# Storing a split projection weight to DRAM one tile sooner in the first token quarter

## The chip, the cores and the metric

The kernel runs on one core of one Trainium2 chip. The metric is device time in microseconds; lower is better. Before the change it takes 2681.71 us, the median of three runs (2680.83 to 2684.74).

## The reference

One decoder layer over 2048 tokens with a width of 1024, in fp32. A combined input projection feeds four gated-DeltaNet heads and four HGRN2 heads; their outputs go through an output projection, then an MLP and an embedding gate. The part that matters here is the projection and what is made of it:

```
hn   = rms_norm(h, pre_mix_norm)
proj = einsum('btd,dc->btc', hn, w_in)          # 1024 x (32 blocks of 128, and 8 decay columns)
qkv  = silu(causal_conv(proj[qkv]))              # gated DeltaNet: q, k, v, z, and decay a, b
f, i, q, g = proj[hgrn]                          # HGRN2: forget, input, query, gate
o_a  = gated_delta_rule(q, k, v, decay, beta)    # 4 heads
o_b  = hgrn2(silu(q), (1 - lb) sigmoid(-f), i, log_f)   # 4 heads
h    = h + rms_norm(concat(o_a, o_b) @ w_out)
h    = h + rms_norm(relu(rms_norm(h) @ w_up)^2 @ w_down)
h    = h + rms_norm(p @ w_ple) * sigmoid(h @ w_gate)
```

## The kernel before, in words

Every fp32 matrix product is done as three products of "split" operands. A tile is split into a rounded copy (ScalarE, ACT, line 167) and the remainder (VectorE, DVE, line 168). A weight block of 1024 x 128 in both parts is a tile `w` of 1 MB in one of three buffers with the tag `whl`; its unsplit form `raw` is 0.5 MB in one of two buffers with the tag `raw`.

The projection and the two mixers run as a list of `works`, four quarters of 512 tokens each. A quarter has 33 works: work 0 is the small `ab` block (decay and beta), and then come eight weight blocks (k, q, v, z, f, i, query, g) for each of four head pairs. Work j is one output tile of 24 matmuls (line 1219), done in three parts of eight. After each part `tick()` runs what the `agenda` holds for that clock: steps of the mixers (`gdn_mixer`, `hgrn_mixer`), whose offsets are lists written out by hand (`A_STEPS`, `B_STEPS`, and `A_FIRST` for the first head). After the last part, `then` moves the product out of PSUM (`conv_silu`, `gate` with its tile `zt`, `fold`).

In the first quarter each weight block is loaded raw (`stage_work`, line 390) and split (`split_work`, lines 167 and 168). The split tile is also stored to DRAM (`keep_work`, which calls `keep`, line 183, tensor `cache_in`). In the three later quarters `split_work` reloads it from there (`reload`, line 188). At the head of step j the order is: split tile j+2, start the raw load of j+3, store tile j. So a `whl` buffer comes free for tile j+3 when PE has used tile j and the store of tile j has landed. The ab tile and the first raw loads are done ahead of the loop.

The order on TensorE (PE) is the program's (`manual_schedule` around the whole), and in this loop SyncE's (SP) too: SP issues all transfers, in one queue and in program order, and waits there for what each needs. The orders on ACT, DVE and GpSimd (POOL) are set by a planner, which weighs readiness by its own cost estimates.

The steps of a DeltaNet head that the prediction names: decay rows `gb` are stored (`gd`, line 640) and read back spread over the partitions (`gf`, line 744). From `gf` come `tail` (755), `e` (761, then 763 on ACT) and further exponentials. `u` goes through DRAM as `ud` (820) and comes back as `sys` (829); the small triangular solves make `xs` (840 to 845), stored as `xd` (850), read back as `xt` (857) and turned into `xn` (859); `psp`, `part`, `pst`, `psd` join the blocks (864 to 900), and `psa`, `psb`, `psc` carry the state `S` (906 to 918). In the HGRN2 head `keys` (1000) and `qk` (997) feed the `at` products (995).

Of the kernel before, what the change touches and what calls it, by code (L numbers as in the profile page):

```python
# [85 lines left out]
def trunk(ctx, tc, x, xT, pT, vecs, w_in, w_ab, gdn_a_log, gdn_dt_bias, w_out, w_up, w_down,  # L86
# [19 lines left out]
    def bank(name, pool=None):  # L106
        return (pool or pm).tile([P, QT], F32, tag="ps", name=name)

    def blk(c):
        return slice(c * P, (c + 1) * P)  # L110
# [69 lines left out]
    def keep(key, w):  # L180

        c = dr.tile([P, 2 * KD * P], F32, name=f"cache_{key}")
        nc.sync.dma_start(c, w.bitcast(F32).rearrange("p h k n -> p (h k n)"))
        cached[key] = c
# [67 lines left out]
    def tok(q):  # L252
        return slice(q * QT, (q + 1) * QT)
# [30 lines left out]
    def stage_ple(i, name, parts=1):  # L284

        raw = wp.tile([P, KD, P], F32, tag="raw", name=f"raw_{name}", bufs=2)
        n = 4 // parts

        def fetch(j):
            nc.sync.dma_start(raw[:, 2 * n * j : 2 * n * (j + 1)].rearrange("p (d k) n -> p d k n", k=2),  # L290
                              w_ple[4 * i + n * j : 4 * i + n * (j + 1)].rearrange("d p k n -> p d k n"))

        def ready(eng):
            w = wp.tile([P, 2, KD, P], F32R, tag="whl", name=f"w_{name}")
            for half in range(2):
                sl = slice(half * KD // 2, (half + 1) * KD // 2)
                split(w[:, :, sl], eng, raw[:, sl])
                if parts > 1:
                    between[half]()
            return w  # L300

        fetch(0)
        between = [lambda: None] * 2
        return (ready, partial(fetch, 1), between) if parts > 1 else ready
# [72 lines left out]
    def tick():  # L377
        for gen in agenda.pop(clock[0], ()):
            next(gen, None)
        clock[0] += 1  # L380

    def half():

        for gen in agenda.pop(clock[0] - 0.5, ()):
            next(gen, None)
# [184 lines left out]
    with mixers as mctx:  # L570
# [51 lines left out]
        def decays(ps, q):  # L622

            if q:
                gb = mt(f"gb_{q}", "gb", 1, (36, QT))
                rows = decay_rows(ps, gb, m2.tile([4, QT], F32, tag="tmp", name=f"sp_{q}"),
                                  m2.tile([4, QT], F32, tag="th", name=f"se_{q}"),
                                  lambda: tc.issue_after(turns[-1]))
                for _ in range(3):
                    next(rows)  # L630
                yield
                next(rows, None)
                gd = dr.tile([4, QT], F32, name=f"gd{q}")
                decay[q] = [gd, None]
                yield
                nc.sync.dma_start(gd, gb[0:4, :])
            else:
                gb, gd = first_gb, dr.tile([4, QT], F32, name="gd0")
                decay[q] = [gd, None]
                nc.sync.dma_start(gd, gb[0:4, :])  # L640
            yield
            back = mt(f"gbb_{q}", "gbb", 1, (36, QT // 2))
            V.tensor_copy(back.rearrange("p (n b i) -> p n b i", b=NB, i=SB), odd_back(gb))
            ps = bank(f"ps_gb_{q}", ph)
            for c in range(NC):
                PE.transpose(ps[:, c * 36 : (c + 1) * 36], back[:, blk(c // 2)] if c % 2 else gb[:, blk(c)],
                             ident[:36, :36])
            gcol = sm.tile([P, NC, 36], F32, tag="gcol", name=f"gcol_{q}", bufs=2)
            V.tensor_copy(gcol.rearrange("p c n -> p (c n)"), ps[:, : NC * 36])
            V.tensor_scalar(gcol[:, :, 4:8], gcol[:, :, 0:4], -1.0, None, ALU.mult)  # L650
            decay[q][1] = gcol

        def urgent(gen):

            done = False
            while not done:
                with tc.high_priority():
                    done = next(gen, gen) is gen
                yield
# [429 lines left out]
        works = []  # L1089

        def at(t, gen, offsets):
            for o in offsets:
                agenda.setdefault(t + o, []).append(gen)

        def call(t, fn):
            def once():
                fn()
                yield
            at(t, once(), (0,))
# [18 lines left out]
        def stage_work(j):  # L1118

            if j < len(works) and works[j][3] == 0:  # L1120
                staged[j] = stage(works[j][0], works[j][2])

        def split_work(j):

            if j < len(works):
                split_w[j] = staged.pop(j)() if j in staged else reload(works[j][1], works[j][0])

        def keep_work(j):
            if works[j][3] == 0:
                keep(works[j][1], split_w[j])  # L1130

        def load_x(q):
# [66 lines left out]
        with tc.manual_schedule(engines={mybir.EngineType.SP}):  # L1199
            assert [w[0] for w in works[:4]] == ["ab0", "4_0_0", "0_0_0", "8_0_0"]  # L1200
            for j, (name, key, src, q, h, then, g, b) in enumerate(works):
                if j:
                    split_work(j + 2)
                if j:
                    stage_work(j + 3)
                if j:
                    keep_work(j)
                ps = bank(f"mm_{name}", pp if j == 2 else None) if j else ps_ab
                w, xt = split_w.pop(j), xts[q]
                terms = []  # L1210
                for k, xk in enumerate(xt):
                    terms += [(w[:, 0, k, :], xk[:, 0, :]), (w[:, 0, k, :], xk[:, 1, :]), (w[:, 1, k, :], xk[:, 0, :])]
                nt = len(terms)
                for s in range(SPT):
                    for i in range(s * nt // SPT, (s + 1) * nt // SPT):
                        if i == (2 * s + 1) * nt // (2 * SPT):
                            half()
                        if j:
                            PE.matmul(ps, *terms[i], start=i == 0, stop=i == nt - 1)  # L1219
                    if s == SPT - 1 and h is None:  # L1220
                        at(clock[0], decays(ps, q) if q else urgent(decays(ps, q)), (0, 2.5, 3, 5) if q else (2, 6))
                    tick()
                    if s == SPT - 1 and h is not None:
                        then(ps, q, h, g, b)

            qs = (2, 3)
            ple = [stage_ple(i, f"pleb{i}") for i in range(2)]
            pts = {q: [operand(ra, pT[blk(k), tok(q)], f"pT{q}_{k}", stage=m2) for k in range(2)] for q in qs}
            ple = [w(V) for w in ple]
            fill = [(q, d) for q in qs for d in range(KD)]  # L1230
            store = None
            at(clock[0], mix_operands(0), (0, 1, 2, 3, 4, 6, 7, 9, 11))
            call(clock[0] + 2, partial(stage_out, 0))
            call(clock[0] + 5, partial(ready_out, 0))
            call(clock[0] + 6, partial(stage_out, 1))
            call(clock[0] + 13, partial(ready_out, 1))
            call(clock[0] + 14, partial(stage_out, 2))
            held = {}
            homes = (("ld", 2), ("tmp", 2), ("rsx", 1), ("ld", 2), ("th", 2))

            def first_outs():

                for j in range(2):
                    ps = held[j] = bank(f"mmo_0_{j}")
                    w = ready.pop(j)
                    for i in range(3 * KD):
                        k, term = i // 3, i % 3
                        PE.matmul(ps, w[:, term // 2, k, :], xin[0][k][:, term % 2, :], start=i == 0, stop=i == 3 * KD - 1)
                        if i % 8 == 7:
                            yield  # L1250

            outs = first_outs()
            while clock[0] <= last or len(held) < 2 or 1 in ready:
                if fill:
                    q, d = fill.pop(0)
                    new = embed_tile(q, d, ple[d // 4], pts[q], m2, *homes[len(fill) % len(homes)])
                    if store:
                        store()
                    store = new
                else:  # L1260
                    if store:
                        store()
                        store = None
                    next(outs, None)
                half()
                tick()
            for _ in outs:
                tick()
# [730 lines left out]
```

## Time and profile before

| | us |
|---|---|
| median of three runs | 2681.71 |
| the profiled execution | 2682.78 |
| its span, first to last instruction | 2681.0 |
| PE busy | 2643.5 (99%) |
| DVE busy | 2023.3 (75%) |
| ACT busy | 1499.5 (56%) |
| POOL busy | 106.4 (4%) |

The first quarter's works run on PE from about 38 to 280 us. All times inside the profile are counted from the span's start. In a line of waits, the three numbers are the total in us, how often, and the longest. In a line of the timeline, the first number is the start, the second the length, and in square brackets stands the engine's idle time just before and what ended it. In a line of windows come the stretch, its length, the busy times of PE, PEld, DVE, ACT and POOL with counts of instructions, the clock granted to PE, the DMA engines' busy share and GB/s.

### The profile page before, as it was taken

Reading aid. Unit: us, or ns where it says so; the run is one execution under the profiler, and the core shown is the slowest. Engines: PE = TensorE matmul, PEld = TensorE weight load, DVE = VectorE, ACT = ScalarE, POOL = GpSimd, SP = SyncE. Lnnn points to the kernel's source line nnn. Section 1 sums busy time; section 2 is a strip of 40 time slices with the busy share of each in tenths; the row PEclk is TensorE's granted clock in tenths of the full one; section 3 lists DMA queues with packets and bytes.
Section 4 is the critical chain, followed back from the end, with each engine's and each line's share of the span. In section 5 each row is a group of like instructions: output and inputs, shape, how many; then the busy total and the mean of one; then the engine's idle time right before and its main releaser. Section 6 shows DMA issues by size and latency. Waiting matters only on the chain.

```text
span 2681.0 us, 38473 instructions
## 1 busy us (share of the span) xinstructions
PE 2643.5 (99%) x12729; PEld 2206.1 (82%) x12729; DVE 2023.3 (75%) x4202; ACT 1499.5 (56%) x3174; POOL 106.4 (4%) x114
## 2 busy tenths in 40 slices
PE   8999999999999999999999999999999999999999
PEld 6888888888888888888888888887888888888887
DVE  6787777777787777478889977757788875668776
ACT  6665655465456456576566655545466664465322
POOL 0000000000000000000000000000000000001000
PEclk9999999999999999999999999999999999999999
DMA  8876777666656665877566676657465655677563
GB/s 282 273 260 216 235 257 231 220 209 243 214 201 222 219 219 176 296 276 276 176 217 219 214 240 222 211 195 252 140 235 178 206 194 191 196 252 254 191 223 133
DMA packets 268311, 594.11 MB, mean 222 GB/s; under 512 B 50250, under 2 KB 54824, under 8 KB 250704
## 3 DMA queue, kind: packets, MB, share of 16 engines
q1 hardware_dynamic: 268112, 591.65, 65.2%
q8 instruction: 101, 1.65, 0.3%
q14 instruction: 98, 0.80, 0.1%
HBM read 427.83 MB, written 163.70 MB: 221 GB/s over the span
## 4 chain that ended last, share of the span: by engine, by line
PE 65%; DVE 17%; DMA 10%; ACT 4%; issue 2%; POOL 1%; SPq 1%; POOLq 0%; DVEq 0%; ACTq 0%
PE u L1286 21%; PE d L1286 20%; PE mm L1219 10%; PE mmg L1286 6%; DVE pr_g L840 3%; PE mmo L1286 2%; DMA sys_g<-ud_g 2%; DVE xs_g L843 2%; DMA ud_g<-u_g 2%; DVE xs_g L845 2%; PE mme L194 1%; DMA rsb_g<-rd_g 1%; DMA da<-sumd 1%; DMA mixT<-mixd 1%; DMA raw_out<-in_w_out_dram 1%
## 5 line engine op out<-in xcount | busy, mean ns | idle before, releaser
L1219 PE MATMUL mm<-xt,w 128*128 128x512 f32 x3072 | 785.1, 401 | 4.1 <-ACT zt_zg L712 3.5
L1219 PEld LDWEIGHTS mm<-xt,w 128*128 128x128 f32 x3072 | 555.2, 189 | 108.1 <-ACT zt_zg L712 3.7
L1286 PE MATMUL d<-db,da 128*128 128x512 f32 x2688 | 611.3, 389 | 1.7 <-DVE db L221 1.6
L1286 PE MATMUL u<-t,wu 128*128 128x512 f32 x2604 | 592.8, 389 | 1.7 <-ACT wu L167 0.8
L1286 PEld LDWEIGHTS d<-db,da 128*128 128x128 f32 x2688 | 504.1, 188 | 108.2 <-DVE db L221 3.6
L1286 PEld LDWEIGHTS u<-t,wu 128*128 128x128 f32 x2604 | 488.5, 188 | 104.3 <-ACT wu L167 1.2
L221 DVE TENSOR_TENSOR db<-db 128x512 fp32r<-128x512 f32 x224 | 159.6, 713 | 70.6 <-ACT db L220 70.0
L220 ACT ACTIVATE db<-db 128x512 fp32r<-128x512 f32 x224 | 140.8, 629 | 78.4 <-DMA db<-hid 76.7
L1675 DVE TENSOR_TENSOR u<-u,u 128x512 f32<-128x512 f32 x224 | 150.2, 680 | 37.1 <-PE u L1286 36.3
L1716 ACT ACTIVATE u<-u 128x512 f32<-128x512 f32 x128 | 80.8, 631 | 171.3 <-DVE u L1675 171.3
L1286 PE MATMUL mmg<-h2T,wg 128*128 128x512 f32 (+1 forms) x792 | 175.1, 383 | 0.3 <-DVE yu L1779 0.2
L1286 PEld LDWEIGHTS mmg<-h2T,wg 128*128 128x128 f32 x792 | 145.4, 188 | 30.1 <-DVE h2T L221 0.6
L1286 PE MATMUL mmo<-mixT,w_out 128*128 128x512 f32 x720 | 164.5, 389 | 0.0
L168 DVE TENSOR_TENSOR da<-da 128x512 fp32r<-128x512 f32 x128 | 94.3, 737 | 86.9 <-ACT da L167 86.6
L1286 PEld LDWEIGHTS mmo<-mixT,w_out 128*128 128x128 f32 x720 | 135.0, 188 | 28.5 <-DMA w_out<-rest 0.6
L167 ACT ACTIVATE da<-da 128x512 fp32r<-128x512 f32 x128 | 80.4, 628 | 134.0 <-DMA da<-sumd 114.6
L840 DVE TENSOR_TENSOR pr_g<-xs_g,sys_g 128x16 f32<-128x16 f32 (+14 forms) x240 | 93.8, 391 | 5.6
L231 POOL TENSOR_TENSOR acc_y<-acc_y,sq_y 128x512 f32<-128x512 f32 x28 | 39.1, 1397 | 1356.1 <-ACT sq_y L230 1356.1
L168 DVE TENSOR_TENSOR wu<-a,wu 128x512 fp32r<-128x512 f32 x124 | 84.7, 686 | 6.5 <-ACT wu L167 6.5
L167 ACT ACTIVATE wu<-a 128x512 fp32r<-128x512 f32 x124 | 73.3, 621 | 24.3 <-DMA a<-in_w_up_dram 21.6
L1717 ACT ACTIVATE u<-u 128x512 f32<-128x512 f32 x128 | 80.3, 628 | 2.9
L168 DVE TENSOR_TENSOR da<-dr,da 128x512 fp32r<-128x512 f32 x96 | 66.2, 689 | 18.1 <-ACT da L167 16.1
(392 smaller groups left out, 3808.3 us busy)
## 6 DMA issues: line engine op xcount, KB each, us to landing
w<-cache_in SPq DMA_DIRECT2D x96, 1024.0 KB
db<-hid SPq DMA_DIRECT2D x224, 256.0 KB
cache_in<-w SPq DMA_DIRECT2D x32, 1024.0 KB
hid<-u SPq DMA_DIRECT2D x128, 256.0 KB
da<-sumd SPq DMA_DIRECT2D x128, 256.0 KB
a<-in_w_up_dram SPq DMA_DIRECT2D x124, 256.0 KB
hid<-ht SPq DMA_DIRECT2D x96, 256.0 KB
dr<-in_w_down_dram SPq DMA_DIRECT2D x96, 256.0 KB
```

The source lines that it names most:

```text
L167: S.activation(t[:, 0], raw, AF.Copy)
L168: eng.tensor_tensor(t[:, 1], raw, t[:, 0], ALU.subtract)
L220: S.activation(t[:, 0], plain(t), AF.Copy)
L221: V.tensor_tensor(t[:, 1], plain(t), t[:, 0], ALU.subtract)
L840: V.tensor_tensor(pr[:, :, :, 0:i], xs[:, None, :, 0:i].broadcast_to([P, 2, GC, i]), sys[:, 0:i, i : i + 2].rearrange("p j two -> p two j" ...
L843: V.tensor_reduce(xs[:, :, i : i + 2].rearrange("p g two -> p two g"), pr[:, :, :, 0 : i + 1], AX.X, ALU.add)
L845: V.scalar_tensor_tensor(xs[:, :, i + 1], xs[:, :, i], sys[:, i, i + 1 : i + 2], xs[:, :, i + 1], ALU.mult, ALU.add)
L1219: PE.matmul(ps, *terms[i], start=i == 0, stop=i == nt - 1)
L1286: PE.matmul(ps, a, b, start=start, stop=stop)
L1675: V.tensor_tensor(c[new], c[old], ps, ALU.add)
L1716: S.activation(c[k], c[k], AF.Relu)
L1717: S.activation(c[k], c[k], AF.Square)
```

## The change

At step j the tile that is stored is j+1 and no longer j; step 1 stores tiles 1 and 2. The place in the step, behind the raw load of j+3, stays. Step 32 stores nothing, since work 33 belongs to the second quarter. The 32 stores, their size and their destinations are the same.

```
         def keep_work(j):
-            if works[j][3] == 0:
+            if j < len(works) and works[j][3] == 0:
                 keep(works[j][1], split_w[j])
...
                 if j:
                     stage_work(j + 3)
                 if j:
-                    keep_work(j)
+                    for i in (1, 2) if j == 1 else (j + 1,):
+                        keep_work(i)
```

More of the change, by code (lines that the diff above doesn't have):

```diff
@@ L1128, in keep_work @@
         def keep_work(j):
-            if works[j][3] == 0:
+            if j < len(works) and works[j][3] == 0:
                 keep(works[j][1], split_w[j])
@@ L1206, in trunk @@
                 if j:
-                    keep_work(j)
+                    for i in (1, 2) if j == 1 else (j + 1,):
+                        keep_work(i)
                 ps = bank(f"mm_{name}", pp if j == 2 else None) if j else ps_ab
```

## The prediction

> **What bounds the kernel now.** I read the page's busy times first, then what TensorE waited for in the first quarter, then the waits on the stores themselves (ScalarE's and SyncE's), and last the single instructions around each wait, by engine.
>
> ```profile
> span 2681.0 us, 38473 instructions
> PE 2643.5 (99%) x12729; PEld 2206.1 (82%) x12729; DVE 2023.3 (75%) x4202; ACT 1499.5 (56%) x3174; POOL 106.4 (4%) x114
> ```
>
> PE is busy for 99% of the span, so an edit is worth what it takes from or adds to PE's waits. The edit touches works 1 to 32 only, PE's time from 38 to about 280 us. PE's waits there, with some room for what follows:
>
> ```profile
> PE mm L1219 <- ACT zt_zg L712: 3.5, 1, 3.5
> PE psa_g L906 <- DVE S_g L918: 1.9, 1, 1.9
> PE pst_g L864 <- issue: 1.1, 1, 1.1
> PE at_h L995 <- ACT keys_h L1000: 0.9, 2, 0.7
> ```
>
> ```profile
> PE kk_g L802 <- ACT y_qg L686: 0.6, 1, 0.6
> ```
>
> These five come to 8.0 us. None names a store or a `w` tile: no store makes PE wait directly. A wait can cost more than its length, since the granted clock (third column from the right) falls behind it:
>
> ```profile
> 68.00:72.00 4.00, 4.00 (x14) 2.99 (x13) 3.13 (x8) 3.74 (x13) 0.00 (x0) 0.57 0.84 262
> 260.00:268.00 8.00, 6.27 (x25) 5.39 (x26) 7.83 (x27) 2.09 (x5) 0.00 (x0) 0.79 0.72 247
> ```
>
> After the 3.5 us wait the loss is 4 x (1 - 0.57) = 1.7 us; after the 1.9 us wait it is 8 x (1 - 0.79) = 1.7 us. The first wait is thus worth 5.2 us, the second 3.6. The stores show up as waits elsewhere:
>
> ```profile
> ACT w L167 <- DMA cache_in<-w: 9.7, 5, 3.3
> ```
>
> ```profile
> SPq L188 <- DMA cache_in<-w: 19.8, 2, 11.7
> ```
>
> ScalarE's split of a tile waits five times until the store of the tile three works earlier has left the buffer (three `whl` buffers). SyncE's reload waits twice for the same reason at the quarter's end.
>
> **The change part by part.** *Steady state (steps 2 to 31).* Each step issues one raw load and one store as before; only the index of the stored tile rises by one. Every transfer on SP's queue between two steps (ud, sys, xd, xt, gf, xs, mixd) has the same 1 MB store ahead of it as before. No instruction is added, and POOL issues no transfer and reads no `w`. The moved store needs DVE's remainder of tile j+1; the raw load just ahead of it, for j+3, waits for that same subtraction to free its buffer (two `raw` buffers), so the store adds no wait. At steps 30 and 31 no raw load stands ahead. There SP comes to the place late, behind a mixer's transfer (step 30) and the loads of the next x (step 31), when the tiles have been split. Cost 0, hidden by SP's wait for the raw buffer.
>
> *Step 1: one store more.* Store 2 now leaves directly behind store 1, not 8 us later. These are SP's rows, a 12 us and a 1 us window (last column GB/s), and the DVE, ACT and PE rows that hang on them:
>
> ```profile
> 39.73 0.91 SPq L183 DMA_DIRECT2D cache_in<-w  x1
> 46.95 0.27 SPq L640 DMA_DIRECT2D gd<-gb  x1
> 48.07 0.33 SPq L390 DMA_DIRECT2D raw<-in_w_in_dram  x1
> 48.46 0.42 SPq L183 DMA_DIRECT2D cache_in<-w  x1
> 49.17 0.32 SPq L744 DMA_DIRECT2D gf_g<-gd  x1
> ```
>
> ```profile
> 36.00:48.00 12.00, 12.00 (x54) 9.94 (x53) 9.36 (x18) 7.69 (x11) 3.41 (x15) 1.00 0.85 289
> 48.00:49.00 1.00, 1.00 (x6) 0.84 (x5) 0.96 (x4) 0.00 (x0) 0.00 (x0) 1.00 0.06 21
> ```
>
> ```profile
> 56.87 0.17 DVE L755 TENSOR_TENSOR tail_g<-gf_g,gcol 128x4 f32<-128x4 f32 x1 [0.75 <-DMA gf_g<-gd]
> 56.95 0.68 DVE L761 TENSOR_TENSOR e_g<-gf_g,cst 128x512 f32<-128x512 f32 x1
> ```
>
> ```profile
> 59.44 1.27 ACT L763 ACTIVATE e_g<-e_g,gcol 128x128 f32<-128x128 f32 x4
> ```
>
> ```profile
> 63.18 1.09 ACT L167 ACTIVATE w<-raw 128x1024 fp32r<-128x1024 f32 x1
> ```
>
> ```profile
> 66.10 0.60 ACT L712 ACTIVATE zt_zg<-mm 128x512 f32<-128x512 f32 x1
> ```
>
> ```profile
> 66.75 2.54 PE L1219 MATMUL mm<-xt,w 128*128 128x512 f32 x8 [3.49 <-ACT zt_zg L712]
> ```
>
> SP itself has room for the extra issue (0.42 us), idle from 40.64 to 46.95. The transfer is 1.05 MB; at the 289 GB/s of that stretch it takes 3.6 us, and the idle microsecond at 48 (share 0.06) absorbs 0.9. Behind it stand gd, raw 5, store 3 and gf_g, so gf_g, which tail_g already waits for, lands about 2.7 us later. Cover: DVE's e_g ends at 57.63 and ACT takes it up at 59.44, a slack of 1.8. The rest, 0.9 us, goes through an ACT that runs from e_g to zt_zg without a break, into PE's longest wait. Bounds: 0 if gd and gf_g slip through; above, the extra store takes 6.3 us (store 9 below, from issue to the split that waited for it), 6.3 - 1.8 = +4.5. I take +0.9, since the 289 GB/s row is of this stretch.
>
> The Trainium skill, "DMA: Bandwidth & Descriptors", section "Queues, rings and completion order", states that each DMA engine consumes descriptors in ring order, though completions need not come in order: a rule against this change. By it gf_g is late as above and the sum stands; were it not so here, the term would be 0 and the sum 0.9 us lower. No row of before separates the two.
>
> *Middle: the five split waits, 9.7 us of ACT.* They end once each store leaves a step sooner. What PE gets:
>
> ```profile
> 95.49 0.33 SPq L390 DMA_DIRECT2D raw<-in_w_in_dram  x1
> 95.86 0.43 SPq L183 DMA_DIRECT2D cache_in<-w  x1
> ```
>
> ```profile
> 102.15 1.06 ACT L167 ACTIVATE w<-raw 128x1024 fp32r<-128x1024 f32 x1 [3.09 <-DMA cache_in<-w]
> ```
>
> ```profile
> 108.69 1.06 ACT L167 ACTIVATE w<-raw 128x1024 fp32r<-128x1024 f32 x1 [2.16 <-DMA cache_in<-w]
> ```
>
> ```profile
> 115.16 0.88 ACT L877 ACTIVATE part<-psp_g 32x64 f32<-32x64 f32 x4
> ```
>
> ```profile
> 116.14 0.68 PE L864 MATMUL pst_g<-xt_g,part 128*128 128x128 f32 x4 [1.06 <-issue]
> ```
>
> PE's 1.06 us at 116.14 is ACT's `part`, ending at 116.04. ACT ran without a break from 108.69 to there; 2.16 us sooner, `part` would not be late. With the 0.2 us second wait on keys_h that gives -1.2. What is late next is the raw load: raw 12 left at 95.49 and had landed by 102.15, no row says when. Bounds: 0 (raw lands with the store, the wait only changes its name) and -1.2. I take -1.2, as no split in the loop shows a wait for raw.
>
> *End: two reloads, 19.8 us of SP.*
>
> ```profile
> 266.55 0.42 SPq L183 DMA_DIRECT2D cache_in<-w  x1
> 278.74 0.32 SPq L188 DMA_DIRECT2D w<-cache_in  x1
> 279.11 0.42 SPq L183 DMA_DIRECT2D cache_in<-w  x1
> 287.64 0.32 SPq L188 DMA_DIRECT2D w<-cache_in  x1
> 288.05 0.38 SPq L850 DMA_DIRECT2D xd_g<-xs_g  x1
> ```
>
> ```profile
> 286.24 0.22 DVE L845 SCALAR_TENSOR_TENSOR xs_g<-xs_g,sys_g 128x4 f32<-128x4 f32 x1
> ```
>
> ```profile
> 296.04 0.45 DVE L859 STREAM_TRANSPOSE xn_g<-xt_g 128x256 f32<-128x256 f32 x1 [2.37 <-DMA xt_g<-xd_g]
> ```
>
> ```profile
> 298.01 0.71 PE L995 MATMUL at_h<-qk_h,keys_h 128*128 128x128 f32 x4 [0.70 <-ACT keys_h L1000]
> ```
>
> ```profile
> 38.30:281.00 242.70, 195.53 (x772) 141.68 (x773) 0.99 0.75 250
> ```
>
> Store 32 now takes the place at 266.55, and none is left at 279.11. The reloads then wait for PE alone. This window over line 1219 counts 772 matmuls until 281; tile 32 is used up with the 768th (32 x 24), one microsecond earlier. So the second reload leaves near 280, some 7 us sooner, so xd_g goes out when xs_g ends (286.46, not 288.05) with no 1 MB reload just ahead of it. xn_g and, behind it in DVE's order, the keys come at least 1.6 us sooner; PE's 0.70 goes. I add 0.2 of the later 0.6 us wait on y_qg: -0.9, bounds 0 and -1.3.
>
> **Sum.** +0.9 - 1.2 - 0.9 = -1.2 us. The profiled execution took 2682.78 us (span 2681.0 and 1.8 around it), 1.1 above the median 2681.71; 2681.6 for it, 2680.5 for the median.
>
> **The rivals.** *A, faster: the order on ACT changes.* Only PE's and SP's orders are written out; ACT's and DVE's come from the planner, whose times for stores and buffers shift. If zt_zg moves ahead of the split at 63.18 and of the decay exponentials, PE's first wait falls under 1.06 us, a length behind which the clock held, and up to 5.2 us go. With middle and end: 2681.71 - 5.2 - 1.2 - 0.9 = 2674.4. For it: that wait is the costliest. Against: zt_zg follows work of earlier program order, and the extra store makes that work later. Had all 9.7 us of ACT waits reached PE, the time would be 2672.0; PE's five waits exclude it but for the two named.
>
> *B, slower: the extra store holds up gf_g.* Place: gd, raw 5, store 3, gf_g. Price at the upper bound: +4.5 on PE, and a second 1.7 us of lowered clock as the wait grows to 8 us; with middle and end at nothing, 2681.71 + 4.5 + 1.7 = 2687.9. It begins to cost once gf_g lands 1.8 us later and outweighs the gains from 1.8 + 2.1 = 3.9 us. For it: gf_g is already waited for. Against: the queue had drained at 48.
>
> *C, no gain: the raw load takes the store's place.* Middle and end 0, the start stays: 2682.6. For it: raw and store leave 0.37 us apart. Against: raw is half the bytes and leaves first.
>
> **How the numbers follow.** Forecast 0.45, C 0.10, A 0.25, B 0.20. A measurement of this kernel can tell about 0.2%, 5.4 us, from no change. Forecast and C lie within it; B is over it in 0.15 and within it in 0.05; A is faster by more. Faster 0.25, same 0.60, slower 0.15. The likeliest case is 2680.5, its own range 2679.2 (start 0, middle -1.2, end -1.3) to 2682.6. The range runs from A's price, 2674.5, to 2687.0, B without its last microsecond; some 0.18 lies outside.
>
> **What would show it.** Right: no split waits on a store in the loop, two `cache_in` stores in a row near 40 us, tail_g's wait up from 0.75 us, zt_zg's start within 1 us of 66.10 plus 0.9, the 1.06 us at pst_g gone, the reloads issued sooner, the second near 280. Wrong: ACT's instructions in another order around zt_zg, PE's wait there below 2 or above 6 us, splits waiting for raw, or PE waits that change after 320 us, where the edit touches nothing.

## The result, and the profile after

| | median us | runs | range |
|---|---|---|---|
| before, same chip | 2682.22 | 22 | 2677.74 to 2688.72 |
| after | 2686.11 | 22 | 2683.33 to 2693.65 |

The ratio is 1.0016, 95% interval 1.001 to 1.0023: the change makes the kernel about 0.16% slower, 3.9 us between the medians. The forecast was 1.2 us faster. The profiled execution of after took 2684.63 us, 1.85 more than that of before.

The page of after shows the same busy time on PE (2643.5 us before):

```profile
span 2682.8 us, 38479 instructions
PE 2643.8 (99%) x12729; PEld 2207.0 (82%) x12729; DVE 2022.8 (75%) x4202; ACT 1500.0 (56%) x3174; POOL 105.0 (4%) x114
```

PE's waits in the first quarter (38 to 320 us) are other ones now. Lines behind the loop's head are one higher than before (L1220 was L1219).

```profile
PE psp_g L864 <- DVE xn_g L859: 4.5, 1, 4.5
PE psc_g L916 <- ACT w_g L913: 1.9, 3, 0.7
PE t_vg L707 <- ACT y_vg L683: 1.6, 1, 1.6
PE at_h L995 <- ACT hist L674: 0.9, 1, 0.9
```

The 3.5 us on zt_zg, the 1.1 at pst_g and the waits on keys_h are gone. A wait of 4.5 us on xn_g, which before had none, has come, and waits on w_g grew from 0.2 to 1.9 us.

The stores do what the change says. SP at the loop's head:

```profile
40.26 1.56 SPq L183 DMA_DIRECT2D cache_in<-w  x2
47.49 0.26 SPq L640 DMA_DIRECT2D gd<-gb  x1
...
52.14 0.32 SPq L744 DMA_DIRECT2D gf_g<-gd  x1
```

Two stores leave together, and gf_g is issued at 52.14 in place of 49.17 us. (All of after's loop runs 0.5 us later from the start: gd is at 47.49, before at 46.95.) No split waits on a store any more; SP's second reload at the quarter's end still waits 5.5 us for one. What the prediction did not reckon with stands on ACT:

```profile
58.25 0.26 ACT L778 ACTIVATE jk_g<-t_kg 128x128 bf16<-128x128 f32 x1
...
59.30 0.66 ACT L794 ACTIVATE q_g<-y_qg 128x512 f32<-128x512 f32 x1
...
61.73 1.28 ACT L763 ACTIVATE e_g<-e_g,gcol 128x128 f32<-128x128 f32 x4
...
64.43 1.06 ACT L167 ACTIVATE w<-raw 128x1024 fp32r<-128x1024 f32 x1
...
66.80 0.42 ACT L683 ACTIVATE y_vg<-acc_vg 128x256 f32<-128x256 f32 x1
...
67.43 0.58 ACT L712 ACTIVATE zt_zg<-mm 128x512 f32<-128x512 f32 x1
```

Before, the exponentials (59.44) came ahead of jk_g and q_g (64.13), and zt_zg (66.10) ahead of y_vg (68.38). The row of before:

```profile
68.38 0.39 ACT L684 ACTIVATE y_vg<-acc_vg 128x256 f32<-128x256 f32 x1
```

Compared instruction by instruction, ACT's order differs in 105 places (its instructions 60 to 457) and DVE's in 229 (77 to 635), all in the first quarter; the order on PE is the same, and that on SP but for the stores. So the planner laid out other orders for the changed program.

The wait on zt_zg went by way of DVE. By the kernel's text the products of v and z hold the two PSUM buffers of their pool (`pm`, line 101), and PE's next tile needs one of them. Here is DVE's last pass of acc_vg, which reads v's product, before and then after:

```profile
67.41 0.74 DVE L677 SCALAR_TENSOR_TENSOR acc_vg<-mm,cols,acc_vg 128x511 f32<-128x511 f32 x1
```

```profile
61.60 0.75 DVE L677 SCALAR_TENSOR_TENSOR acc_vg<-mm,cols,acc_vg 128x511 f32<-128x511 f32 x1
```

Before, zt_zg was done with z's buffer first, at 66.70, and PE waited for it. After, DVE is done with v's at 62.35, and PE starts the tile at 63.55 without a wait, before zt_zg has run.

PE on its way through the first quarter (before, then after):

```profile
88.97 0.60 PE L707 MATMUL t_ih<-cst,iT_h 128*128 128x128 f32 x4
...
112.62 0.61 PE L864 MATMUL psp_g<-xn_g,um 128*128 128x128 f32 x4
112.98 2.09 PE L1219 MATMUL mm<-xt,w 128*128 128x512 f32 x8
...
117.10 0.39 PE L801 MATMUL kk_g<-y_kg 128*128 128x128 f32 x2
```

```profile
67.27 0.85 PE L707 MATMUL t_vg<-cst,y_vg 128*128 128x128 f32 x4 [1.63 <-ACT y_vg L683]
...
86.14 0.60 PE L707 MATMUL t_ih<-cst,iT_h 128*128 128x128 f32 x4
...
115.16 1.19 PE L864 MATMUL psp_g<-xn_g,um 128*128 128x128 f32 x4 [4.45 <-DVE xn_g L859]
116.00 3.76 PE L1220 MATMUL mm<-xt,w 128*128 128x512 f32 x8
...
121.23 0.39 PE L801 MATMUL kk_g<-y_kg 128*128 128x128 f32 x2
```

At t_ih after is 2.8 us ahead. When it begins to wait for xn_g (115.16 - 4.45 = 110.71, against 112.62) it is 1.9 ahead, 0.9 having gone in the wait on hist. The wait turns that into 2.5 behind. The next stretch, psp_g to kk_g, takes 6.07 us in place of 4.48, though the 1.06 at pst_g is gone: eight matmuls last 3.76 us where eight lasted 2.09 before, and the granted clock (third column from the right) is low:

```profile
116.00:120.00 4.00, 4.00 (x13) 0.50 1.01 390
```

At kk_g after is 4.1 us behind (3.6 if each is counted from its loop's start). Part of this comes back near 260 us, where before had its 1.9 us wait on S_g and a clock of 0.79; after has 1.00 there from 260 to 268 us.

Why xn_g is late is seen on DVE. The triangular solve is a chain of xs_g steps, each of which needs the one before. These are groups of DVE's work from its first to its last link (79.5 to 100.2 us before, 78.9 to 103.1 after), before first:

```profile
L168 DVE TENSOR_TENSOR w<-raw,w 128x1024 fp32r<-128x1024 f32 x3 | 3.6, 1216 | 0.0
...
L677 DVE SCALAR_TENSOR_TENSOR acc_kg<-mm,cols,acc_kg 128x509 f32<-128x509 f32 x1 | 0.7, 740 | 0.0
```

```profile
L168 DVE TENSOR_TENSOR w<-raw,w 128x1024 fp32r<-128x1024 f32 x4 | 4.9, 1221 | 0.0
...
L677 DVE SCALAR_TENSOR_TENSOR acc_kg<-mm,cols,acc_kg 128x509 f32<-128x509 f32 (+2 forms) x3 | 2.2, 739 | 0.0
```

One more split remainder (1.2 us), two more passes of acc_kg (1.5 us) and three more att and qk_h steps (1.2 us) now stand between the links of xs_g. So xd_g leaves at 103.21 us in place of 100.21, and xt_g follows. Then xn_g itself stands behind the ssk_g, rk_g and cc_g steps and acc_vg in DVE's order (before, then after):

```profile
111.00 0.44 DVE L859 STREAM_TRANSPOSE xn_g<-xt_g 128x256 f32<-128x256 f32 x1
```

```profile
112.83 0.16 DVE L786 TENSOR_TENSOR cc_g<-rk_g 128x4 f32<-128x4 f32 x1 [1.12 <-POOL rk_g L163]
...
114.58 0.43 DVE L859 STREAM_TRANSPOSE xn_g<-xt_g 128x256 f32<-128x256 f32 x1
```

Before, xn_g ended at 111.44, only 1.2 us ahead of PE. After, it ends 3.6 us later and PE comes 1.9 us sooner: 3.6 + 1.9 - 1.2 = 4.3 of the 4.5 us.

### The profile page after: what moved, and what is told of

The parts are those of the page before. It is cut to its first block, busy times and chain, and to the rows that moved or that the text cites. A ratio compares the mean times of both kernels' runs of the same rounds, so it can differ in the third digit from the quotient of the medians.

```text
span 2682.8 us, 38479 instructions
## 1 busy us (share of the span) xinstructions
PE 2643.8 (99%) x12729; PEld 2207.0 (82%) x12729; DVE 2022.8 (75%) x4202; ACT 1500.0 (56%) x3174; POOL 105.0 (4%) x114
## 4 chain that ended last, share of the span: by engine, by line
PE 70%; DVE 14%; DMA 6%; ACT 4%; issue 4%; POOL 1%; SPq 1%; POOLq 0%; DVEq 0%; ACTq 0%
PE u L1287 21%; PE d L1287 20%; PE mm L1220 12%; PE mmg L1287 6%; PE mmo L1287 3%; DVE pr_g L840 2%; DVE xs_g L843 2%; DMA sys_g<-ud_g 1%; PE mme L194 1%; DMA ud_g<-u_g 1%; DVE xs_g L845 1%; DMA da<-sumd 1%; PE at_h L995 1%; POOL acc_y L231 1%; DVE xt L168 1%
## 5 line engine op out<-in xcount | busy, mean ns | idle before, releaser
L1220 PE MATMUL mm<-xt,w 128*128 128x512 f32 x3072 | 784.3, 401 | 0.0
L1220 PEld LDWEIGHTS mm<-xt,w 128*128 128x128 f32 x3072 | 555.0, 189 | 103.2
```

## The experiments

Two theories stood against each other. O: the new order on ACT and DVE loses the time, and the moved stores by themselves gain a little. S: the moved stores lose it, and the order is a bystander. An order is held by a list: for each engine the instructions of the first quarter in their wanted order, each tied behind the one before it. Nothing else in the kernel's text changes.

```
+PINNED = {"Activation": "55 1 19 ...", "DVE": "68 1 -3 ...", "Pool": "20 -2 ..."}
+def pin(tc): ...            # tie each listed instruction behind the one before it
         trunk(tc, *args)
+        pin(tc)
```

| run | stores | order | median us | before beside it | ratio, 95% interval |
|---|---|---|---|---|---|
| x1 | new | old | 2679.82 | 2681.47 | 0.9995 (0.9987 to 1.0004) |
| x2 | old | new | 2689.44 | 2681.47 | 1.0031 (1.0019 to 1.0043) |
| x3 | shifted, the double at step 2 | new | 2683.95 | 2681.47 | 1.001 (1.0002 to 1.0019) |
| x4 | only store 2 early | old | 2679.79 | 2681.47 | 0.9999 (0.999 to 1.0008) |
| after again | new | new | 2685.80 | 2681.47 | 1.0011 (1.0002 to 1.002) |
| x6 | new | new in the first head only | 2677.48 | 2681.47 | 0.9983 (0.9974 to 0.9992) |
| x8 | new | new, xn_g 11 places up | 2685.14 | 2681.47 | 1.0009 (1.0 to 1.0018) |
| x9 | new | new up to 120 us | 2685.74 | 2681.47 | 1.0009 (1.0001 to 1.0018) |
| x12 | new | head, DVE's solve, 14 of ACT | 2687.03 | 2680.66 | 1.0033 (1.002 to 1.0045) |
| x13 | new | head, ACT up to 125 | 2678.43 | 2680.66 | 0.9993 (0.9984 to 1.0002) |
| x14 | old | new in the first head only | 2678.74 | 2680.66 | 0.9998 (0.9988 to 1.0008) |

x1 to x4 ran on one chip, after again, x6, x8 and x9 on a second, x12 to x14 on a third, each beside runs of before. x2 and x12 have five executions, the others eleven or twelve.

**x1, the stores alone, with the order of before.**

> The changed kernel's stores, with the order of ScalarE's, VectorE's and GpSimd's instructions pinned to that of the kernel before. Theory O (the planner's new order makes the difference, the stores are worth about a microsecond): PE's 4.5 us wait on xn_g is gone, the 3.5 us wait on zt_zg is back, time 2680 to 2683. Theory S (the stores themselves cost, through the extra megabyte at step 1 and raw loads that land late): 2685 to 2687.

**x2, the order alone, with the stores of before.**

> The stores of the kernel before, with the order of ScalarE, VectorE and GpSimd pinned to that of the changed kernel. Theory O: the wait on zt_zg is gone, a wait of 4 to 5 us on xn_g stands in PE, and the time is 2685 to 2688. Theory S: 2681 to 2683.

Leading waits of PE in x1, then the first in x2:

```profile
PE mm L1220 <- ACT zt_zg L712: 3.5, 1, 3.5
PE mm L1220 <- ACT qk_h L940: 0.8, 1, 0.8
...
PE psa_g L906 <- DVE S_g L918: 0.6, 1, 0.6
PE pst_g L864 <- issue: 0.6, 1, 0.6
```

```profile
PE psp_g L864 <- DVE xn_g L859: 6.6, 1, 6.6
```

With the old order xn_g's wait does not exist and zt_zg's is back. Without the moved stores the new order is worse still: 2689.44, above the 2685 to 2688 that was expected. Against each other: the stores take 1.7 us off the medians with the old order and 3.6 with the new one (2689.44 against the 2685.80 of after again); the order adds 8.0 us with the old stores and 6.0 with the new ones (after again against x1). The 3.6 and the 6.0 are taken across two chips, on which before has the same median, so they are rough. S falls: x1's interval ends at 1.0004. That x1 alone is faster than before is not shown (its interval holds 1).

**x3 and x4, the two halves of the change.** In x3 step 2 stores tiles 2 and 3 and step 1 only tile 1; in x4 only store 2 is early, and from tile 3 on all is as before. The planner is free in both.

```
x3: for i in (1,) if j == 1 else (2, 3) if j == 2 else (j + 1,):
x4: for i in (1, 2) if j == 1 else () if j == 2 else (j,):
```

> Step 1 stores tile 1 alone, step 2 stores tiles 2 and 3, and from step 3 on the change stands; the planner is free and gives the changed kernel's order. Theory O: as the changed kernel, 2685 to 2687, with gf_g landing as before. If the double store at step 1 (the prediction's rival B) were the cause: 2681 to 2683.

> Only store 2 moves, to step 1 behind store 1; all other stores stay at their old steps. The planner is free and gives the order of the kernel before. The prediction's first term by itself: gf_g lands 2.7 us later, zt_zg and PE behind it 0.9 us later (0 to 4.5), time 2682 to 2684. Rival B: 2686 to 2688.

x3 gets the same ACT and DVE orders as after, x4 those of before. x3 has the 4.3 us wait on xn_g (and 2683.95, under the 2685 to 2687 expected), x4 the 3.5 on zt_zg. So it is the shift from step 2 on that tips the planner, not the second store at step 1. x3 still has one step with two stores; whether the shift would do it without any is not shown.

x4 does not test what its expectation says. Step 2 stores nothing there, so no store stands between gd and gf_g, and tail_g does not wait for gf_g at all. It shows that store 2 can leave early at no cost that can be measured (0.9999). What an extra store ahead of gf_g does is seen in x1 alone.

**x6, the first head's new order without the rest.** ACT's instructions 60 to 82, DVE's 77 to 97 and POOL's 21 and 22 in the new order, all else in the old one.

> The stores of after. ACT, DVE and POOL take the planner's new order only in the first head's stretch (ACT positions 60 to 82, DVE 77 to 97, POOL 21 and 22: the decay exponentials, y_vg, zt_zg and what stands between them); everywhere else the order of before. Theory O (the order decides, and its first part gains while its second part loses): zt_zg's 3.5 us wait is gone, t_vg waits 1.6 us on y_vg as in after; PE then reaches the psp products some 3 us earlier, and since xn_g keeps its old place (near 110.5 us), psp waits 1 to 2 us for it in place of 4.5. 2681.5 - 3.5 - 1.7 (clock) + 1.6 + 1.5 - 1 (splits) = about 2678, between 2676 and 2680. Theory S (the moved stores lose, the order does not): 2686, as after. If the first head's new order is itself what costs: 2684 or more.

```profile
PE mm L1220 <- ACT qk_h L940: 1.8, 1, 1.8
PE t_vg L707 <- ACT y_vg L683: 1.6, 1, 1.6
```

2677.48: the fastest version, 0.17% under before and 8.3 us under after on the same chip. psp_g does not wait at all (1 to 2 us had been expected); the time went to qk_h, 1.8 us. The loss of the new order thus lies behind its head. Whether the head's order gains by itself is what x14 asks.

**x8, xn_g moved up; x9, the later part of the new order undone; after once more.**

> After as it is, but xn_g's first transpose (114.58 us in after) is moved up eleven places in DVE's order, to directly behind the split's remainder that ends near 110.7 us: ahead of the ssk_g, rk_g and cc_g steps (1.12 us of waiting for POOL's rk_g among them), qk_h and acc_vg. Theory O: the transpose starts near 110.7, PE's wait at psp_g falls from 4.5 to 0.6 us, and with the clock that falls behind it 4 to 5 us go: 2681 to 2682. If the chain of transfers (xd_g, xt_g) and not DVE's order makes xn_g late: the transpose shows a wait of 2 us or more for xt_g, PE still waits over 2.5 us, and the time is 2684 or more. Theory S: 2686, whatever xn_g does.

x8's rows on DVE and PE, and its clock:

```profile
111.41 0.45 DVE L859 STREAM_TRANSPOSE xn_g<-xt_g 128x256 f32<-128x256 f32 x1 [1.98 <-DMA xt_g<-xd_g]
```

```profile
112.00 0.78 PE L864 MATMUL psp_g<-xn_g,um 128*128 128x128 f32 x4 [2.19 <-DVE xn_g L859]
...
117.00 0.68 PE L864 MATMUL pst_g<-xt_g,part 128*128 128x128 f32 x4 [0.89 <-issue]
```

```profile
112.00:116.00 4.00, 4.00 (x12) 0.57 0.96 363
```

> The stores of after; the new order in the first head and through the first group of psp products (ACT positions below 126, DVE below 225, to about 120 us), the order of before behind that. It tells whether the loss is the stretch up to 120 us or what follows it. Theory O as read from after's waits (4.5 us at xn_g before 120 us; behind it 1.9 us in three waits on w_g and 1.2 on S_h and S_g, against 0.7 and 1.4 with the old order): 2684 to 2686, the loss lies ahead of 120 us. If the later stretch holds the loss: 2682 or less. Theory S: 2686.

> The changed kernel itself, for a second profile and its time beside the three others on the same chip. Both theories: 2686, between 2684 and 2687.5, with the 4 to 5 us wait of psp_g on xn_g. The clock behind that wait may differ from one profile to the next.

The place of xn_g in DVE's order is not the cause by itself: moved up, it waits 1.98 us for its own transfer, PE still waits 2.2 us, the clock falls here too (0.57), and pst_g loses 0.9. The late end of the solve ahead of it stays. The median is only 0.7 us under that of after again, though PE's wait is half as long; the profiled execution is the shortest of x8's eleven (2682.22), so this profile does not explain the median. x9 gives all of after's loss (2685.74) with the new order up to 120 us alone; its wait on xn_g is 7.5 us. So nothing is lost on balance behind 120 us. After again gives 2685.80, its profile a wait of 4.3 us.

**x12, x13 and x14, the stretch taken apart.** x6 plus DVE's new order from 120 to 194 (with the 14 ACT instructions it needs); x6 plus ACT's new order from 83 to 125; x6 with the stores of before.

> The kernel with only the first head's stretch in the new order, plus DVE's new order of the triangular solve up to xn_g (DVE positions 120 to 194) and of the 14 ACT instructions (positions 101 to 114) that DVE's order needs. ACT's qk_h ahead of the exponentials and of the split (positions 83 to 92) stays old. If DVE's new order of the solve is what loses (splits, acc_kg and the att steps between the links of xs_g, and xn_g last): xs_g ends 3 us later than with the old order, xn_g's transpose starts at 113 to 117 us, PE waits 4 to 7 us for it, 2684 to 2687. If ACT's order loses: xn_g near 110, 2677 to 2680.

> The kernel with only the first head's stretch in the new order, plus ACT's new order from 83 to 125 (qk_h ahead of the second head's exponentials, then splits, acc_kg, keys_h); DVE's solve and xn_g stay in the old order. If DVE's order loses: xn_g near 110 us, PE waits under 2 us for it, 2676 to 2680, and PE's 1.8 us wait on qk_h goes as in after. If ACT's order loses: 2683 or more.

> The stores of before with the new order in the first head alone: what is the first head's order worth without the moved stores, and what do the stores add to it? Theory O with a gain of the stores of 1.7 us (as between before and x1): 2679 to 2680 against 2677.5 with the moved stores; splits wait for stores again by some 10 us of ACT, the reload by 20 us of SP. If the whole gain of the order goes through the moved stores: 2681 or more. If the stores add nothing: 2677.5.

PE's first wait in x12, and its longest in x13, which has none on xn_g:

```profile
PE psp_g L864 <- DVE xn_g L859: 6.8, 1, 6.8
```

```profile
PE t_vg L707 <- ACT y_vg L683: 1.6, 1, 1.6
...
PE at_h L995 <- ACT hist L674: 0.7, 1, 0.7
```

DVE's order from the solve to xn_g is the cause: x12 loses as much as x2 (1.0033 and 1.0031), x13 is not slower than before. x12 has the order of x9 on DVE, and x13 that of x9 on ACT, with x12's 14 ACT instructions among them; so the loss comes with DVE's new order and stays away without it. The profiles say the same: counted from the loop's first matmul, PE reaches kk_g after 76.4 us in x6 and 76.9 in x13, but after 83.6 in x9 and 84.7 in x12 (78.6 in before, 82.2 in after). The splits, acc_kg and att steps inside the solve and what follows it up to xn_g were not taken apart further than by x8. x13 shows that qk_h's wait goes with ACT's new order, yet 2678.43 beside its before (0.9993) is no better than x6 (0.9983). In x14 the splits wait for stores for 12.6 us and SP's reload for 17.3, and the ratio is 0.9998: the first head's new order alone shows no gain, with the moved stores it shows 0.17%. The medians, 1.9 and 4.0 us under their before, agree with some 2 us from the stores, but the intervals of x14 and x6 overlap.

## Why the prediction was wrong

**The step that failed** is the one that kept the orders of ACT and DVE. The sum was worked out on the instructions of before in their old order; that the planner might lay them out anew stood in rival A alone, with a price read from one wait of before (zt_zg), so only as a gain. The planner did it, but not with the effect that A gave it: by the medians its new order cost 6.0 us (after again against x1) to 8.0 us (x2 against before), more than the 1.7 to 3.6 us that the stores gave. It had to be asked as well which instruction without a wait before could become the last: PE did not wait for xn_g, but xn_g was only 1.2 us ahead of it (111.44 and 112.62). Some 3.5 us more from the first to the last link of the solve, and a PE ahead by 1.9 us, used that up. Losses from a new order were left without a bound. That 2686.11 lies inside the stated range is luck: the range reached so high for rival B, which did not happen.

**Rival A**: its place was right, its mechanism not. zt_zg did not move up; it starts at 67.43, later than before. PE's tile no longer waits for it, since v's buffer is free first; the t_vg behind that tile waits 1.63 us for y_vg. What that is worth beside the moved stores is x6: 4.0 us by the medians, where A said 7.3 with all else.

**Rival B** fell: in x1, which has the extra store and the old order, gf_g comes 1.0 us later and zt_zg no later. **Rival C** was half right: the raw load took over part of the waits, 3.5 of 9.7 us of ACT in x1:

```profile
ACT w L167 <- DMA raw<-in_w_in_dram: 3.5, 2, 3.0
```

**The terms, against x1, which has the order they assumed.** Start, +0.9: sized wrong. tail_g waits longer for gf_g and ACT starts e_g no later, counted from the loop's own start (x1's runs 0.48 us later; 59.44 and 66.10 before):

```profile
58.34 0.17 DVE L755 TENSOR_TENSOR tail_g<-gf_g,gcol 128x4 f32<-128x4 f32 x1 [1.76 <-DMA gf_g<-gd]
```

```profile
59.92 1.27 ACT L763 ACTIVATE e_g<-e_g,gcol 128x128 f32<-128x128 f32 x4
...
66.58 0.60 ACT L712 ACTIVATE zt_zg<-mm 128x512 f32<-128x512 f32 x1
```

gf_g landed 1.0 us later (1.76 - 0.75), not 2.7, and the 1.8 us of slack covered it: the term is 0. The Trainium skill, "DMA: Bandwidth & Descriptors", section "Queues, rings and completion order", states that descriptors are consumed in ring order; the later issue of gf_g, which waits for gd behind the stores, agrees with it, and the delay that reached tail_g was 1.0 us.

Middle, -1.2: mechanism right, too large. pst_g's 1.1 us became 0.6, and the waits on keys_h are gone, but PE waits 0.8 for qk_h.

End, -0.9: right in kind, but the reloads were to wait for PE alone, and the second does not. The first row takes both together; they leave at 268.32 and 277.34, and ahead of the second SP waits 6.9 us for a store and then 1.8 for PE. xd_g does leave when xs_g ends:

```profile
268.32 9.34 SPq L188 DMA_DIRECT2D w<-cache_in  x2
284.72 0.32 SPq L850 DMA_DIRECT2D xd_g<-xs_g  x1
```

```profile
SPq L188 <- DMA cache_in<-w: 6.9, 1, 6.9
```

Of PE's waits there keys_h and y_qg go, and S_g's falls from 1.9 to 0.6, which was not foreseen. The sum, -1.2, stands beside the measured -1.7 (interval -3.5 to +1.1): it agrees, but with terms that erred both ways, and an interval that holds 0 does not confirm it. Nothing in x1 speaks against the steady state's "cost 0"; but it was just this shift, as x3 shows, that changed the planner's order.

What stays open: why the planner's estimates tip, since only its orders were compared; and the new order with the first head alone put back, which was not tried. x9 waits 7.5 us where after waits 4.5, yet from psp_g to kk_g it takes 4.80 us and after 6.07; so at kk_g x9 is only 1.3 us later than after, each counted from its loop's start, and the medians do not tell the two apart.

## What to carry to other kernels

Where a planner sets the order on some engines, moving a transfer is two changes: the transfer, and another order. Compare the instruction orders per engine first, and price each chain that comes later by its slack to its consumer, not by its waits before, since a chain without any wait may have only a few us to give. To judge the edit itself, hold the old order and time the two apart; a stretch of the new order may be worth keeping (x6, with the moved stores, is 0.17% under before).

## What the hardware showed

The same wait cost very different clock in different runs. The 3.5 us wait on zt_zg stands in x1 and x4 alike; the clock behind it, x1 first:

```profile
68.00:72.00 4.00, 3.81 (x19) 1.00 0.73 207
```

```profile
64.00:68.00 4.00, 1.01 (x2) 0.73 0.33 138
68.00:72.00 4.00, 4.00 (x13) 0.50 0.82 250
72.00:76.00 4.00, 4.00 (x18) 0.91 0.45 160
```

The clock is not lowered in x1. By the windows it takes 4 x (1 - 0.57) = 1.7 us in before and 4 x (0.27 + 0.50 + 0.09) = 3.4 us in x4, but part of the latter falls into the wait itself (PE starts again at 66.99), where it costs nothing. What the clock cost is read from the start of the tile behind the wait to t_ih: 20.8 us in x1 (88.19 - 67.23, less a wait of 0.19), 22.2 in before (88.97 - 66.75) and 23.2 in x4 (90.20 - 66.99), so nothing, 1.4 and 2.4 us. The prediction's price of 5.2 us for that wait, from one profile, is 3.5, 4.9 or 5.9 us by this count. The Trainium skill, "TensorE: Matmul & The Clock Gate", section "What's actually happening", states that the activity window runs freely, so that the point of change varies from run to run; these three agree. It puts the drop behind about 3.4 us of idleness; x8's 2.2 us wait was followed by a drop all the same, and where the two differ the measurement decides. Runs of one kernel spread over up to 12 us (after again: 2679.82 to 2691.62), and the profiled execution of x1 is the shortest of its twelve, that of x4 the second longest; so a single profile says where time goes, and only the medians what it is worth.
